# Sums of the middle norm behind the last product, two weight splits earlier, and the pre-FFN norm's steps one slot later, in a streaming encoder layer

## The chip, the cores and the metric

The kernel runs on one core of a Trainium2 chip. The core has a matrix engine (PE, with its weight loads listed apart as PEld), a vector engine (DVE), a scalar engine (ACT), a further engine called POOL, and SP, which only issues the DMAs here. Each engine takes its own instructions in a fixed order and waits on semaphores for the others. The metric is the device time of one execution in microseconds (us); lower is better.

## The reference, cut to what matters

One layer of a hybrid encoder runs on 256 + 64 = 320 tokens with 2048 features. The change lies between the output projection of the mixer and the up-projection of the feed-forward part:

```
x = x + rmsnorm(jnp.concatenate([a_out, b_out], axis=-1) @ w_out, g_post_mix)
h = rmsnorm(x, g_pre_ffn)
gu, ffn_buf = causal_dwconv(h @ w_up, ffn_buf, w_ffn_dw, b_ffn_dw)
gate, up = jnp.split(gu, 2, axis=-1)
x = x + rmsnorm((jax.nn.silu(gate) * up) @ w_down, g_post_ffn)
```

`rmsnorm` divides each token by the root of the mean of its squares over the 2048 features and multiplies by a gain per feature.

## The kernel before

**Layout.** Features lie on the 128 partitions, tokens along the free dimension (T = 320), so the 2048 features are 16 blocks of 128 x 320. Each fp32 weight tile `w` is split in two: ACT casts it to `whi` (L217), DVE subtracts to get `wlo` (L218), and the same is done with the activations. A product is three matmuls: `whi` with the high part of x, `whi` with its low part, `wlo` with the high part (L233, L234, L237 in `block_matmul`; L1067 to L1069 in `second`). Loaded tiles `w` rotate through three buffers (`wst`), so a load waits until the `wlo` of the load three earlier is done; the split tiles rotate through three pairs (`wsp`).

**Output projection.** Its contraction of 16 blocks is cut in 11 + 5. The first 11 of output blocks 0 to 14 are done before the region of the change. The loop that begins at L1084 then goes through output blocks n = 0 to 15: it loads and splits the 640 columns of `w_out2` for the block, runs 15 matmuls (`second`), and `evacuate` adds the result to `m[n]` on DVE (L1080), squares it on ACT into `sq` (L1040), multiplies by the gain g2 on ACT (L1083), and adds `sq` to the running sum `acc` on DVE (L1042). Block 15, the last product, is done whole: 33 matmuls from two loads of `w_out1` (768 and 640 columns) and 15 from `w_out2`, 48 in all. Its own square is not added to `acc`; it stays in `sq`.

**Up-weight sets.** The first up-projection group (`up_group`, L1163) needs eight sets of weights, each a load of 128 x 1024 with a split. Three of them are loaded inside the loop (`upr`, at n in (3, 6, 10)) and split inside it (`upw`, at n in (6, 10, 14)); the split is placed, on ACT and on DVE, behind that engine's newest instruction from the split of the same block's `w_out2`. Those loads have two buffers of their own, the split tiles three. Five more sets follow behind the loop.

**Mid norm.** `rstd([acc, last])` sums over the partitions with matmuls that have the data as weights and a column of ones as moving operand: three for `acc` and three for `sq` (L259; each is two passes in the trace). DVE (L264) and POOL (L265) make the reciprocal root, `rstd_rows` spreads it over the partitions (L272), and `keep_warm` puts dummy matmuls (L280) around that. Then DVE and ACT update x1 and make the two parts of the next input block by block.

**Other norm.** The norm before the feed-forward part is applied behind the up-projection, to its result. `second_norm` is a job of two steps: the sums of `acc` (16 squares of x1), and then `rb2`, the spread root, which ACT copies out of PSUM (L1178). Jobs advance at every 20th matmul that `block_matmul` counts; `start(second_norm(), 68, 1)` makes the first step due 68 matmuls on, and the second is due 12 after it. The first seven up-projection results wait in PSUM for `rb2`: four from `up_group`, and blocks 2, NFB + 2 and 3 (48 matmuls each) that PE runs meanwhile. DVE empties them with L1195 and L1196 into `fbuf`.

**What sets the order.** A scheduler lays out each engine's instructions at build time, by priorities (`tc.high_priority`) and by a model of when operands are ready; `tc.issue_after(i)` holds what is in its scope behind instruction i. At run time the order on each engine is fixed.

Of the kernel before, what the change touches and what calls it, by code (L numbers as in the profile page):

```python
# [17 lines left out]
P = 128  # L18
# [4 lines left out]
T = TP + TS  # L23
# [77 lines left out]
def trunk_kernel(ctx, tc, ins, outs):  # L101
    nc = tc.nc
    V, S, G, PE = nc.vector, nc.scalar, nc.gpsimd, nc.tensor
# [32 lines left out]
    def start(gen, wait, g=0, t=0):  # L136
        job = [dense[1] + wait, gen, g, t, []]
        jobs.append(job)
        return job
# [5 lines left out]
    def newest(engine, n0):  # L145
        return next((i for i in reversed(nc.cur_bb.bb.instructions[n0:]) if i.engine == engine), None)
# [45 lines left out]
    def pv(name, a=None, b=None):  # L192
        o, w = PAR[name]
        if a is None:
            return par[:, o:o + w]
        return par[:, o + a:o + (a + 1 if b is None else b)]

    def cv(name, n=P, m=P):
        o, _ = CST[name]
        return cst[0:n, o:o + m] if o < NCST1 else cst2[0:n, o - NCST1:o - NCST1 + m]  # L200
# [20 lines left out]
    def load_split(src, width, pool=None):  # L221
        with tc.high_priority(offset=boost[0]):
            return split_w(load_dma(src), width, pool)

    def block_matmul(ps, src, rhs, nks, final=True, first=True):
        nk = sum(nks)
        k0 = 0
        for nk_part in nks:
            hi, lo = load_split(src[:, k0 * P:(k0 + nk_part) * P], nk_part * P)
            for j in range(nk_part):  # L230
                xh, xl = rhs(k0 + j)
                wh = hi[:, j * P:(j + 1) * P]
                tick(PE.matmul(ps, wh, xh, start=(first and k0 + j == 0), stop=False))  # L233
                tick(PE.matmul(ps, wh, xl, start=False, stop=False))  # L234
            for j in range(nk_part):
                xh, xl = rhs(k0 + j)
                tick(PE.matmul(ps, lo[:, j * P:(j + 1) * P], xh, start=False, stop=(final and k0 + j == nk - 1)))  # L237
            k0 += nk_part
# [15 lines left out]
    def rstd(accs, pool=None, between=None):  # L254
        pool = pool or ps_g
        pst = pool.tile([P, 512], F32, tag=pool.name[-1], name="pst")
        for i, a in enumerate(accs):
            for c, o in enumerate((0, 128, 192)):
                mm = PE.matmul(pst[:, c:c + 1], a[:, o:o + P], cv("ones", P, 1), start=(i == 0 and c == 0),  # L259
                          stop=(i == len(accs) - 1), skip_group_check=True)  # L260
            if between is not None:
                between(i, mm)
        rr = small.tile([P, 3], F32, tag="rr", name="rr")
        V.tensor_scalar(rr, pst[:, 0:3], 1.0 / D, EPS, ALU.mult, ALU.add)  # L264
        G.tensor_tensor(rr, rr, nhalf[:, 0:3], ALU.pow)  # L265
        return rr, mm
# [30 lines left out]
    def hx(k):  # L297
        return hi_t[k], lo_t[k]
# [17 lines left out]
    with tc.tile_pool(name="xp", bufs=1) as xp:  # L316
# [25 lines left out]
        with tc.high_priority(offset=PRI_E):  # L342
            keep_warm(psw, NWARM)

            last = {}
# [42 lines left out]
        for k0 in range(0, KB, 2):  # L388
            hi, lo = pre[k0 // 2]
            for ks in ((k0,), (k0 + 1,)) if k0 < 4 else ((k0, k0 + 1),):  # L390
                for wt in (hi, lo):
                    for k in ks:
                        for i, b in enumerate(FIRST):
                            ps = ready[b][:, 0:T]
                            o = (k - k0) * FW + i * P
                            w = wt[:, o:o + P]
                            xh, xl = hx(k)
# [4 lines left out]
        def first_norm():  # L402
            rr, _ = rstd([ssum[:, 0, :], ssum[:, 1, :]])
            yield 36, 1, 0
            S.copy(rb, rstd_rows(rr)[0])

        job = start(first_norm(), 24, 1)
# [598 lines left out]
    def bx(k):  # L1006
        return b_hi[KORDER[k]], b_lo[KORDER[k]]

    m = []
    for n in range(KB - 1):  # L1010
        psm = ps_p.tile([P, 512], F32, tag="p", name="psm")
# [15 lines left out]
    acc = None  # L1027
# [23 lines left out]
    def up_load(kk, pool=None):  # L1051
        with tc.high_priority(offset=boost[0]):
            return load_dma(up_src[:, :, kk * 256:(kk + 1) * 256], pool)

    def up_split(w, pool=None):
        with tc.high_priority(offset=boost[0]):
            return split_w(w, HALF, pool)

    upw, upr = [], []
    nk2 = KB - K1  # L1060

    def second(n, psm, w, js):
        hi, lo = w
        for j in js:
            xh, xl = bx(K1 + j)
            o = j * P
            PE.matmul(psm, hi[:, o:o + P], xh, start=(j == 0 and n < KB - 1), stop=False)  # L1067
            PE.matmul(psm, hi[:, o:o + P], xl, start=False, stop=False)
            PE.matmul(psm, lo[:, o:o + P], xh, start=False, stop=(j == nk2 - 1))  # L1069

    last = held = None

    def evacuate(n, psm, whole):
        nonlocal last, held
        with tc.high_priority(offset=PRI_E):
            if whole:
                m.append(act.tile([P, T], F32, tag=f"hl{n}", name=f"m{n}"))
                src = psm[:, 0:T]
            else:
                V.tensor_tensor(m[n], m[n], psm[:, 0:T], ALU.add)  # L1080
                src = m[n]
            last = square_acc(n, src)
            held = S.activation(m[n], src, AF.Identity, scale=pv("g2", n)).ins  # L1083

    opened = {}
    for n in range(KB):
        with ExitStack() as e:
            if n == 2:
                e.enter_context(tc.issue_after(flush))
            mark = len(nc.cur_bb.bb.instructions)  # L1090
            w2 = load_split(ins["w_out2"][n], nk2 * P)
        if n in (3, 6, 10):
            upr.append(up_load(len(upr), urp))
        if n in (6, 10, 14):
            with ExitStack() as e:
                for x in (mybir.EngineType.Activation, mybir.EngineType.DVE):
                    e.enter_context(tc.issue_after(newest(x, mark)))
                upw.append(up_split(upr[len(upw)], ugp))
        nc.sync.dma_start(x1[:, n:n + 1, :], ins["x"][:, n:n + 1, :])
        if n == KB - 1:  # L1100
            nc.sync.dma_start(fpar, ins["fpar"])
        whole = n == KB - 1
        pool = (ps_p, ps_t)[n // 2 % 2]
        psm = pool.tile([P, 512], F32, tag=pool.name[-1], name="psm2")
        if whole:
            block_matmul(psm[:, 0:T], ins["w_out1"][n], bx, (6, 5), False)
        if n == 0:
            opened[0] = psm, w2
            second(n, psm[:, 0:T], w2, range(nk2 - 1))
            continue  # L1110
        if n == 1:
            second(n, psm[:, 0:T], w2, range(nk2 - 1))
            second(0, opened[0][0][:, 0:T], opened[0][1], (nk2 - 1,))
            second(n, psm[:, 0:T], w2, (nk2 - 1,))
        else:
            second(n, psm[:, 0:T], w2, range(nk2))
        for n, psm in ((0, opened[0][0]), (1, psm)) if n == 1 else ((n, psm),):
            evacuate(n, psm, whole)
    boost[0] = 0
# [1 line left out]
    hi2, lo2 = [], []  # L1121
    with tc.high_priority(offset=PRI_E):
        psw = ps_p.tile([P, 512], F32, tag="p", name="psw")
        rr, mm = rstd([acc, last])
        keep_warm(psw, 5, mm)
        rb1, mm = rstd_rows(rr)
        keep_warm(psw, 10, mm)
        split = None
        for k in range(KB):
            if k % 2 == 1 and 1 < k < 13:  # L1130
                with ExitStack() as e:
                    if k < 7:
                        e.enter_context(tc.issue_after(split))
                        e.enter_context(tc.issue_after(held))
                    upw.append(up_split(up_load(len(upw))))
            with ExitStack() as e:
                if 0 < k < 4:
                    e.enter_context(tc.issue_after(added))
                V.tensor_tensor(m[k], m[k], rb1, ALU.mult)
            added = V.tensor_tensor(x1[:, k, :], x1[:, k, :], m[k], ALU.add).ins  # L1140
            g = pv("g3", k)
            hi2.append(act.tile([P, T], F32R, tag=f"hh{k}", name=f"hi2_{k}"))
            lo2.append(act.tile([P, T], F32R, tag=f"hl{k}", name=f"lo2_{k}"))
            S.activation(hi2[k], x1[:, k, :], AF.Identity, scale=g)
            split = V.scalar_tensor_tensor(lo2[k], x1[:, k, :], g, hi2[k].bitcast(F32), ALU.mult, ALU.subtract).ins
# [29 lines left out]
    def second_norm():  # L1175
        rr, _ = rstd([acc])
        yield 12, 1, 0
        S.copy(rb2, rstd_rows(rr)[0])  # L1178

    boost[0] = PRI_W  # L1180
    job = start(second_norm(), 68, 1)
    for b in (2, NFB + 2, 3):
        first[b] = ps_g.tile([P, 512], F32, tag="g", name="psu")
        block_matmul(first[b][:, 0:T], ins["w_up"][2 * (b % NFB) + b // NFB], hx2, (8, 8))
# [60 lines left out]
    with tc.high_priority(offset=PRI_E):  # L1245
        last = square_acc(KB - 1, held_y[:, 0:T])
# [13 lines left out]
    rr, mm = rstd([acc, last], ps_p, lambda i, mm: residuals(2 * i, mm))  # L1260
    rb3, mm = rstd_rows(rr, ps_p)
# [10 lines left out]
    for step in PLAN_Y.split():  # L1272
        how, ks = step[0], step[1:]
        n = 2 if len(ks) == 4 else 1
# [96 lines left out]
```

## Time and profile before

| what | value |
|---|---|
| median of three runs | 1484.64 us (1484.1 to 1485.72) |
| the profiled execution | 1484.99 us |
| its span, first to last instruction | 1483.2 us, so 1.79 us lie around it |
| granted PE clock, mean | 0.999 of full speed |
| DVE, ACT, POOL busy | 67%, 49%, 15% of the span |
| HBM read, written | 215.33 MB, 7.12 MB |

The profile has a page of sums and the trace behind it. A row of the timeline gives the start, the duration, the engine, the line of the kernel, the operation, the tiles (out<-in), the shape and a count of like instructions that are merged in the row; in brackets stands how long the engine was idle before and who ended it. Matmuls are pipelined: a row of 0.31 us overlaps the next, so the distance between starts is what a matmul costs. In the chain of waits, a row is start, duration and piece.

### The profile page before, as it was taken

How to read it: one execution, taken by the hardware profiler on the slowest of the kernel's cores; microseconds unless marked ns; L12 is line 12 of the kernel's file. 1: busy time of each engine (PE TensorE's matmuls, PEld its weight loads, DVE VectorE, ACT ScalarE, POOL GpSimd, SP SyncE). 2: the span in 40 equal slices, each digit the busy share in tenths (PEclk: the TensorE clock that was granted, in tenths of full speed). 3: DMA queues.
4: the chain of work that ended last, by engine and by line, in shares of the span. 5: the costliest groups of instructions: out<-in, count | busy, mean ns of one | idle time of the engine just before them, and what ended most of it. 6: DMA issues, size and time to landing. Idle time of an engine off the chain costs nothing.

```text
span 1483.2 us, 27308 instructions
## 1 busy us (share of the span) xinstructions
PE 1474.4 (99%) x10625; PEld 1454.0 (98%) x10626; DVE 993.7 (67%) x1812; ACT 731.9 (49%) x1355; POOL 229.0 (15%) x390
## 2 busy tenths in 40 slices
PE   9999999999999999999999999999999999999998
PEld 9999999999999989999999999999999999999997
DVE  6779888889988778765346666445666445666554
ACT  7674656655554746544334444334444334444453
POOL 0110101021010001322002222002322001223101
PEclk9999999999999999999999999999999999999999
DMA  8435453545445734444554444454444455444453
GB/s 295 140 115 155 158 162 114 153 150 149 127 126 172 231 107 143 157 145 130 149 174 146 153 151 127 146 163 164 147 150 140 137 150 172 148 156 143 136 148 119
DMA packets 98281, 224.22 MB, mean 151 GB/s; under 512 B 18792, under 2 KB 39528, under 8 KB 98152
## 3 DMA queue, kind: packets, MB, share of 16 engines
q1 hardware_dynamic: 98008, 222.45, 47.3%
q8 instruction: 83, 1.36, 0.4%
q14 instruction: 46, 0.38, 0.1%
q10 hardware_dynamic: 144, 0.03, 0.0%
HBM read 215.33 MB, written 7.12 MB: 150 GB/s over the span
## 4 chain that ended last, share of the span: by engine, by line
PE 95%; DVE 2%; ACT 2%; issue 1%; DMA 1%; POOL 0%; DVEq 0%; ACTq 0%; POOLq 0%
PE psu L237 13%; PE psu L234 13%; PE psu L233 13%; PE psdn L233 7%; PE psdn L234 7%; PE psdn L237 7%; PE psq L233 3%; PE psq L234 3%; PE psq L237 3%; PE psu L1163 2%; PE psm L237 2%; PE psm L233 2%; PE psm L234 2%; PE psv L233 1%; PE psgate L233 1%; PE psgate L237 1%
## 5 line engine op out<-in xcount | busy, mean ns | idle before, releaser
L217 ACT CAST whi<-w 128x1024 fp32r<-128x1024 f32 (+2 forms) x440 | 412.4, 940 | 481.7 <-PE psu L234 166.2
L218 DVE TENSOR_TENSOR wlo<-w,whi 128x1024 fp32r<-128x1024 f32 (+2 forms) x440 | 476.7, 1084 | 191.5 <-ACT whi L217 122.3
L233 PE MATMUL psu<-hi,whi 128*128 128x320 f32 x1344 | 397.0, 309 | 0.0
L234 PE MATMUL psu<-lo,whi 128*128 128x320 f32 x1344 | 396.9, 309 | 0.0
L233 PEld LDWEIGHTS psu<-hi,whi 128*128 128x128 f32 x1344 | 252.3, 188 | 0.0
L234 PEld LDWEIGHTS psu<-lo,whi 128*128 128x128 f32 x1344 | 252.3, 188 | 0.0
L237 PE MATMUL psu<-hi,wlo 128*128 128x320 f32 x1344 | 224.4, 309 | 0.0
L237 PEld LDWEIGHTS psu<-hi,wlo 128*128 128x128 f32 x1344 | 203.9, 188 | 0.0
L234 PE MATMUL psdn<-gl,whi 128*128 128x320 f32 x660 | 195.9, 310 | 0.0
L1197 POOL COPY nffn<-fbuf 128x2 f32<-128x2 f32 x88 | 100.5, 1142 | 586.8 <-DVE fbuf L1195 583.7
L1195 DVE TENSOR_TENSOR fbuf<-psu,rb 128x256 f32<-128x256 f32 x88 | 37.3, 424 | 169.0 <-PE psu L237 169.0
L233 PE MATMUL psdn<-gh,whi 128*128 128x320 f32 x480 | 142.8, 309 | 0.0
L234 PEld LDWEIGHTS psdn<-gl,whi 128*128 128x128 f32 x660 | 123.9, 188 | 0.3
L233 PE MATMUL psq<-hh,whi 128*128 128x320 f32 x352 | 105.9, 314 | 0.0
L234 PE MATMUL psq<-hl,whi 128*128 128x320 f32 x352 | 104.1, 309 | 0.0
L233 PEld LDWEIGHTS psdn<-gh,whi 128*128 128x128 f32 x480 | 90.1, 188 | 0.0
L237 PE MATMUL psdn<-gh,wlo 128*128 128x320 f32 x480 | 89.9, 309 | 0.0
L237 PEld LDWEIGHTS psdn<-gh,wlo 128*128 128x128 f32 x480 | 75.3, 188 | 0.0
L233 PEld LDWEIGHTS psq<-hh,whi 128*128 128x128 f32 x352 | 66.1, 188 | 0.5 <-issue 0.2
L234 PEld LDWEIGHTS psq<-hl,whi 128*128 128x128 f32 x352 | 66.1, 188 | 0.2
L563 DVE SCALAR_TENSOR_TENSOR cvt<-ub,par,cvt 128x320 f32<-128x320 f32 x120 | 65.2, 544 | 0.1
L1240 DVE TENSOR_TENSOR y<-y,psdn 128x320 f32<-128x320 f32 x45 | 22.0, 488 | 58.7 <-PE psdn L237 58.7
(356 smaller groups left out, 2473.8 us busy)
## 6 DMA issues: line engine op xcount, KB each, us to landing
w<-in_w_up SPq DMA_DIRECT2D x176, 512.0 KB
w<-in_w_in SPq DMA_DIRECT2D x88, 512.0 KB
w<-in_w_down SPq DMA_DIRECT2D x64, 384.0 KB
w<-in_w_down SPq DMA_DIRECT2D x64, 320.0 KB
w<-in_w_out SPq DMA_DIRECT2D x32, 320.0 KB
w<-in_w_out SPq DMA_DIRECT2D x16, 384.0 KB
w<-in_w_first SPq DMA_DIRECT2D x6, 512.0 KB
wtp<-wsp SPq DMA_DIRECT2D x4, 640.0 KB
```

The source lines that it names most:

```text
L217: S.copy(hi[:, 0:width], w[:, 0:width])
L218: V.tensor_tensor(lo[:, 0:width], w[:, 0:width], hi[:, 0:width].bitcast(F32), ALU.subtract)
L233: tick(PE.matmul(ps, wh, xh, start=(first and k0 + j == 0), stop=False))
L234: tick(PE.matmul(ps, wh, xl, start=False, stop=False))
L237: tick(PE.matmul(ps, lo[:, j * P:(j + 1) * P], xh, start=False, stop=(final and k0 + j == nk - 1)))
L563: return lambda: V.scalar_tensor_tensor(acc, x, w, acc, ALU.mult, ALU.add)
L1163: PE.matmul(pss[i][:, 0:T], wt[:, o:o + P], x, start=(k == 0 and n == 0), stop=(k == KB - 1 and n == 2))
L1195: V.tensor_tensor(buf[:, 2:258], psu[:, 0:TP], rb2[:, 0:TP], ALU.mult)
L1197: G.tensor_copy(nffn[:, b, 0, :], buf[:, 256:258])
L1240: V.tensor_tensor(y[:, n, :], y[:, n, :], psd[:, 0:T], ALU.add)
```

## The change

Three edits. The first sums of the mid norm (those of `acc`) are held behind the last matmul of the last product. The third load inside the loop moves from n = 10 to 9, the second and third split from n = 10 and 14 to 9 and 12. The other norm's first step is due 84 matmuls on and not 68.

```diff
@@ in second(n, psm, w, js)
-            PE.matmul(psm, lo[:, o:o + P], xh, start=False, stop=(j == nk2 - 1))
+            mm = PE.matmul(psm, lo[:, o:o + P], xh, start=False, stop=(j == nk2 - 1))
+        return mm
@@ in the loop over n
-        if n in (3, 6, 10):
+        if n in (3, 6, 9):
             upr.append(up_load(len(upr), urp))
-        if n in (6, 10, 14):
+        if n in (6, 9, 12):
...
-            second(n, psm[:, 0:T], w2, range(nk2))
+            mm = second(n, psm[:, 0:T], w2, range(nk2))
@@ the mid norm
-        rr, mm = rstd([acc, last])
+        with tc.issue_after(mm.ins):
+            rr, mm = rstd([acc, last])
@@ the other norm
-    job = start(second_norm(), 68, 1)
+    job = start(second_norm(), 84, 1)
```

**First place: PE, in the last product (`psm_6790`) and at its end.** The difference, in which `pst` is the PSUM tile of the mid norm's sums:

```order
 L237 MATMUL psm_6790<-bh_2360,wlo 128x320
 L237 MATMUL psm_6790<-bh_3468,wlo 128x320
-L259 MATMUL pst<-cst,acc 128x1 x3
 L237 MATMUL psm_6790<-bh_4386,wlo 128x320
 L237 MATMUL psm_6790<-bh_4977,wlo 128x320
@@ -3200,4 +3199,5 @@
 L1068 MATMUL psm_6790<-bl_6325,whi 128x320
 L1069 MATMUL psm_6790<-bh_6324,wlo 128x320
+L259 MATMUL pst<-cst,acc 128x1 x3
 L259 MATMUL pst<-cst,sq 128x1 x3
```

The three sums of `acc` leave their place behind the 14th of the last product's 48 matmuls and stand behind the 48th, directly ahead of the sums of `sq`.

**Second place: ACT, in the loop, around the third set.** `m_6037`, `m_6089`, `m_6150`, `m_6216` are the results of blocks 9, 10, 11 and 12; a cast of 128x640 is a block's `w_out2`, that of 128x1024 the third up-weight set. Before:

```order
L1083 ACTIVATE m_6089<-m_6089,par 128x320
L217 CAST whi<-w 128x640
L217 CAST whi<-w 128x1024
L1040 ACTIVATE sq<-m_6150 128x320
L1083 ACTIVATE m_6150<-m_6150,par 128x320
L217 CAST whi<-w 128x640
L1040 ACTIVATE sq<-m_6216 128x320
L1083 ACTIVATE m_6216<-m_6216,par 128x320
L217 CAST whi<-w 128x768
```

Now:

```order
L217 CAST whi<-w 128x640
L217 CAST whi<-w 128x1024
L1040 ACTIVATE sq<-m_6037 128x320
L1084 ACTIVATE m_6037<-m_6037,par 128x320
L217 CAST whi<-w 128x640
L1040 ACTIVATE sq<-m_6089 128x320
L1084 ACTIVATE m_6089<-m_6089,par 128x320
L217 CAST whi<-w 128x640
L1040 ACTIVATE sq<-m_6150 128x320
L1084 ACTIVATE m_6150<-m_6150,par 128x320
L217 CAST whi<-w 128x640
L1040 ACTIVATE sq<-m_6216 128x320
```

The third set's cast stands two blocks earlier: behind the cast of `w_out2` of block 12, ahead of the square of block 9. Between the set and the first cast of the last product (128x768) there are four squares now, and two before. DVE's `wlo` rows move in the same way, and the second set's stand one block earlier on both engines. On SP, the load of `fpar` (128x528) moves ahead of the `w_out2` load of block 13; no other load changes its place.

**Third place: PE and ACT, at the other norm.** The rows with `hi_8` and up to `hi_15` in them end block NFB + 2, those from `hi_0` begin block 3. PE before:

```order
L233 MATMUL psu<-hi_14_7002,whi 128x320
L259 MATMUL pst<-cst,acc 128x1 x3
L234 MATMUL psu<-lo_14_7003,whi 128x320
L233 MATMUL psu<-hi_15_7008,whi 128x320
L234 MATMUL psu<-lo_15_7009,whi 128x320
L237 MATMUL psu<-hi_8_6954,wlo 128x320
```

PE now:

```order
L237 MATMUL psu<-hi_13_6996,wlo 128x320
L237 MATMUL psu<-hi_14_7002,wlo 128x320
L237 MATMUL psu<-hi_15_7008,wlo 128x320
L259 MATMUL pst<-cst,acc 128x1 x3
L233 MATMUL psu<-hi_0_6888,whi 128x320
L234 MATMUL psu<-lo_0_6889,whi 128x320
```

The sums stand 11 matmuls later, at the end of block NFB + 2. The spread (`psb`, L272) stood at that end; it now stands 20 matmuls behind the sums, inside block 3. ACT around the copy of `rb2`, before:

```order
L1040 ACTIVATE sq<-x_6336 128x320
L217 CAST whi<-w 128x1024
L1178 COPY rb_6855<-psb 128x320
L1199 ACTIVATE cg<-fbuf_7012,fpar 128x322
L1199 ACTIVATE cu<-fbuf_7013,fpar 128x322
L217 CAST whi<-w 128x1024
```

ACT now:

```order
L1040 ACTIVATE sq<-x_6336 128x320
L217 CAST whi<-w 128x1024 x2
L1180 COPY rb_6855<-psb 128x320
L1201 ACTIVATE cg<-fbuf_7012,fpar 128x322
L1201 ACTIVATE cu<-fbuf_7013,fpar 128x322
```

One more weight cast stands ahead of the copy now. On DVE, the `wlo` that stood directly behind the other norm's `rr` (L264) stands directly ahead of it.

## The prediction, as it was put on record

> **What bounds the kernel now.** I read the page first, then the chain of waits, then the timeline of PE around each edit.
>
> ```profile
> PE 95%; DVE 2%; ACT 2%; issue 1%; DMA 1%; POOL 0%; DVEq 0%; ACTq 0%; POOLq 0%
> ...
> 624.43 1.17 PE psu L237 x8
> 627.95 1.17 PE psu L237 x8
> ```
>
> The first line, from the page, gives the chain that ends last by engine: 95% of it is PE. So a change is worth what it takes from PE's waits and from PE's own instructions on that chain. The other two, from the chain in order of time, give the cost of one matmul: the groups begin 24 matmuls apart (8 of L237, 16 of L233 and L234), and 3.52 us / 24 = 0.147 us. Any larger distance between two starts is a loss. Behind 583 us PE's timeline keeps this pace up to the last norm, so what PE gains before 583 us it keeps to the end. The losses that the edits can reach are four.
>
> The first is inside the last product:
>
> ```profile
> 523.32 0.46 PE L237 MATMUL psm<-bh,wlo 128*128 128x320 f32 x2
> 524.39 0.83 PE L259 MATMUL pst<-cst,acc 128*128 128x1 f32 x6 [0.62 <-DVE acc L1042]
> 525.08 0.68 PE L237 MATMUL psm<-bh,wlo 128*128 128x320 f32 x3
> 525.75 0.31 PE L233 MATMUL psm<-bp,whi 128*128 128x320 f32 x1
> ```
>
> PE reaches the sums of `acc` and waits for DVE. From 523.32 to 525.75 stand six matmuls (two, three, and one that I leave out), 0.88 us of work; it took 2.43 us. **1.55 us** are lost: about 0.78 of waiting, 0.69 for the six passes, 0.08 for getting back to pace.
>
> The second and third are waits for split weights, at the start of the last product and inside block 11:
>
> ```profile
> 520.73 0.31 PE L1069 MATMUL psm<-bh,wlo 128*128 128x320 f32 x1
> 521.46 0.41 PE L233 MATMUL psm<-bh,whi 128*128 128x320 f32 x1 [0.42 <-ACT whi L217]
> ...
> 521.85 0.31 PE L233 MATMUL psm<-bh,whi 128*128 128x320 f32 x1
> ...
> 512.03 0.31 PE L1068 MATMUL psm<-bl,whi 128*128 128x320 f32 x1
> ...
> 512.52 0.31 PE L1067 MATMUL psm<-bp,whi 128*128 128x320 f32 x1
> ```
>
> From 520.73 to 521.85 are three steps, 0.44 us, and it took 1.12: **0.68** lost to ACT's cast of the first part of `w_out1`. From 512.03 to 512.52 are two steps in 0.49 us: **0.20** lost, to the `wlo` of block 11.
>
> The fourth is at the other norm's sums:
>
> ```profile
> 576.43 0.31 PE L233 MATMUL psu<-hi,whi 128*128 128x320 f32 x1
> 576.97 0.83 PE L259 MATMUL pst<-cst,acc 128*128 128x1 f32 x6 [0.23 <-DVE acc L1042]
> 577.66 0.39 PE L234 MATMUL psu<-lo,whi 128*128 128x320 f32 x1
> ```
>
> The sums begin 0.54 us behind the matmul ahead of them, so **0.39** is waiting; their own 0.69 us stays wherever they stand.
>
> **The change part by part. First edit: the sums of `acc` behind the last product.** The 1.55 us inside the product go. In exchange six passes stand between the last matmul and the sums of `sq`. Those wait for ACT's square anyway, and the end of the kernel has the same sequence already in the new form:
>
> ```profile
> 530.00 0.31 PE L1069 MATMUL psm<-bh,wlo 128*128 128x320 f32 x1
> 530.84 0.83 PE L259 MATMUL pst<-cst,sq 128*128 128x1 f32 x6 [0.53 <-ACT sq L1040]
> ...
> 1467.39 0.60 PE L237 MATMUL psy<-gp,wlo 128*128 128x320 f32 x3
> 1467.83 0.72 PE L259 MATMUL pst<-cst,acc 128*128 128x1 f32 x6
> 1468.52 0.83 PE L259 MATMUL pst<-cst,sq 128*128 128x1 f32 x6
> ```
>
> In the middle, without the passes between, the sums of `sq` start 0.84 us behind the last matmul. At the end the third matmul of its row starts at 1467.39 + 2 x 0.147 = 1467.68, the six passes of `acc` follow, and those of `sq` start at 1468.52: again 0.84. The square hides the six passes. If it hid none, 0.69 us would come back; I take 0. `acc` itself was ready at 524.39, and the last product ends past 527 in any case: no new wait. Gain **1.55**, at least 0.86.
>
> **Second edit: the sets.** No instruction is added; two splits move, by one block and by two, the load for the third moves in the code but not in SP's order, and on SP `fpar` passes the `w_out2` load of block 13. What bounds this stage is how far DVE and ACT lag behind PE:
>
> ```profile
> 510.60 0.48 DVE L1042 TENSOR_TENSOR acc<-acc,sq 128x320 f32<-128x320 f32 x1
> 512.13 0.48 DVE L1042 TENSOR_TENSOR acc<-acc,sq 128x320 f32<-128x320 f32 x1
> ...
> 511.52 0.47 ACT L1040 ACTIVATE sq<-m 128x320 f32<-128x320 f32 x1 [0.51 <-DVE m L1080]
> 513.11 0.47 ACT L1040 ACTIVATE sq<-m 128x320 f32<-128x320 f32 x1
> ...
> 500.48 1.22 DVE L218 TENSOR_TENSOR wlo<-w,whi 128x1024 fp32r<-128x1024 f32 x1
> 501.62 0.48 DVE L1080 TENSOR_TENSOR m<-m,psm 128x320 f32<-128x320 f32 x1
> ```
>
> A block costs DVE 1.53 us and ACT 1.59 when they run without a break, and PE 15 x 0.147 = 2.20. So each block makes good 0.6 us of lag, and a set, 1.14 us on DVE, costs two blocks. The chain shows that lag at the last product:
>
> ```profile
> 515.87 1.67 ACT whi L217 x2
> ...
> 519.62 0.48 ACT sq L1040
> ...
> 520.59 0.82 ACT whi L217
> ```
>
> The pair at 515.87 is the cast of block 14's `w_out2` and the third set; from there DVE and ACT hand work to each other without a pause until the cast that PE waits for, at 520.59. PE wants it done at 520.88 - 0.20 = 520.68, so begun by 519.84: it is 0.75 too late. With the set two blocks earlier there are two more blocks to recover in, 1.2 us, which puts the cast near 519.4. Going through the new order step by step, with the distances that these engines kept in the trace, I get 511.75 for the third set, 513.66, 515.85 and 517.44 for the casts of blocks 13 to 15 and 519.2 for this one (an estimate): 0.6 us to spare. The second set falls into a hole:
>
> ```profile
> 507.75 1.68 ACT L217 CAST whi<-w 128x640 fp32r<-128x640 f32 x2 [1.42 <-DMA w<-in_w_out]
> ```
>
> ACT idles 1.42 us there for a load; now the set's cast fills that time, and the `wlo` of block 11, behind which the set no longer stands, is done more than 1 us before PE needs it. The cast also needs its load:
>
> ```profile
> 514.09 3.70 SPq L210 DMA_DIRECT2D w<-in_w_out  x3
> ...
> 515.00:518.50 3.50, 3.50 (x26) 3.50 (x25) 3.21 (x5) 3.44 (x7) 0.00 (x0) 1.00 0.71 204
> ```
>
> The three issues are block 15's 320 KB, then 384 KB and 320 KB of `w_out1`. From 515.0 to 518.5 the DMAs moved 3.5 x 204 = 714 KB, as much as the first two together (721 in the same unit), so the 384 KB were in shortly behind 518.5. In the new order its issue stays at about 515.6, behind the `wlo` of block 13. Gain 0.68 + 0.20 = **0.88**; with the load late, as in the first rival, nothing.
>
> **Third edit: the other norm's steps.** The sums move behind 11 more matmuls, 1.6 us; `acc` was ready at 576.97 and PE now asks at 576.58 + 1.61 = 578.2. Gain **0.39**; 0 if DVE is later than before. The spread stands 20 matmuls behind the sums, 2.9 us, time in which DVE and POOL finish `rr` even with a `wlo` ahead of it on DVE (rows of the last rival). PE's count of instructions is the same.
>
> **Sum.** 1.55 + 0.88 + 0.39 = 2.82 us. The profiled execution took 1484.99, so 1482.17; it lies 0.35 above the median of the three runs, so against that median 1484.64 - 2.82 = **1481.8**, 0.19% less.
>
> **The rivals.** *The last product's weights stay late.* `fpar`, 264 KB, now goes ahead of block 13's load:
>
> ```profile
> 502.87 4.80 DMA w<-in_w_out
> ...
> 509.36 0.33 SPq L210 DMA_DIRECT2D w<-in_w_out  x1
> ...
> 509.00:513.80 4.80, 4.80 (x33) 4.60 (x32) 4.45 (x8) 4.19 (x9) 0.02 (x1) 1.00 0.83 275
> ```
>
> At 275 GB/s those 270 kB take 0.98 us. A `w_out2` load has taken up to 4.80 us under such traffic; with 0.98 more, block 13's would land at 515.1, 1.5 us behind my step for its cast. The casts behind it then slip by 0.85 us, and the issue of the 384 KB, which waits for that block's `wlo`, by 1.0; of the 0.88, 0.3 to 0.7 come back. Against it: the burst ended near 513.8 with both loads in it, so in either order the later one is in by then. Time 1482.1 to 1482.5, about 1482.4; chance 0.20. The Trainium skill, page "DMA: Bandwidth & Descriptors", section "Queues, rings and completion order", says that each DMA engine consumes descriptors in ring order; by that rule block 13's load stands behind all of `fpar`, which speaks for this rival, and no row here shows the two apart.
>
> *The sets collide.* They stand three blocks apart now and not four; three blocks make good 1.8 us, a set costs 1.14 on DVE, but if a load also makes ACT wait there, PE waits at block 13 or 14 instead, and with a later `acc` the 0.39 may go too. Only the first edit counts then: 1484.64 - 1.55 = 1483.1; chance 0.12.
>
> *Slower: the copy of `rb2` comes too late.* The seven results in PSUM are freed only behind it.
>
> ```profile
> 578.38 1.05 ACT L217 CAST whi<-w 128x1024 fp32r<-128x1024 f32 x1 [2.76 <-PE psu L234]
> 579.88 0.43 ACT L1178 COPY rb<-psb 128x320 f32<-128x320 f32 x1 [0.45 <-PE psb L272]
> ...
> 580.75 0.42 DVE L1195 TENSOR_TENSOR fbuf<-psu,rb 128x256 f32<-128x256 f32 x1
> ...
> 586.73 0.31 PE L233 MATMUL psu<-hi,whi 128*128 128x320 f32 x1
> ```
>
> At 586.73 PE begins the block that needs the first of those banks again. DVE freed it at about 581.4. In the new order the spread comes at 581.9 by the old clock, and ACT has one more cast ahead of the copy, which waits for PE to finish with a `whi` tile at about 581.6 and takes 1.05: the copy starts near 582.6 and the bank is free near 583.7, 2.6 us ahead of PE (586.73 - 0.39 = 586.3). PE begins to wait if the copy slips by 2.6 us more, and the kernel is slower than before once it slips by 2.6 + 2.8 = 5.4. Only a weight load that holds up the extra cast could do that; with as much as 8 us of slip the time is 1487. Chance 0.04.
>
> **How the numbers follow.** The forecast, all three gains, has 0.64 and its own range 1481.0 to 1482.5, since single runs before lie from 0.54 below to 1.08 above their median. The range takes in the first rival and the second, with some of that spread: 1481.0 to 1483.5. A measurement of this kernel can tell about 0.2%, 2.97 us, from no change, which puts the bound at 1481.67, only 0.13 below the forecast. Nearly half of the forecast's chance lies beyond it: faster 0.30, the rest and the two middle rivals make the same 0.66, slower 0.04.
>
> **What would show it.** In the profile of the changed kernel: no wait in the last product and six passes of `acc` right behind its last matmul, with the sums of `sq` still 0.84 behind that matmul (first edit); the first matmul of the last product 0.147 behind block 14 (second edit; if not, the row names ACT or a DMA, and that decides between the first two rivals); the other norm's sums 0.147 behind the L237 ahead of them; the block of 586.73 without a wait and 2.8 us earlier. I am wrong if any of these waits stands, or if PE shows a new one above 0.2 us before 600 us.

## The result and the profile after

| what | before | after |
|---|---|---|
| median of 13 runs each | 1484.74 us (1483.92 to 1485.89) | 1481.83 us (1481.32 to 1482.82) |
| profiled execution, its span | 1484.99, 1483.2 us | 1481.38, 1479.6 us |

The ratio is 0.9981, 95% interval 0.9973 to 0.9988: 2.91 us less. The predicted time was 1481.8. The interval lies wholly below 1: the gain is clear of no change, and far below 2%.

The chain that ends last, by engine, from the page of the changed kernel:

```profile
PE 97%; ACT 1%; DVE 1%; DMA 0%; POOL 0%; issue 0%; SPq 0%; DVEq 0%
```

It was 95% PE before, and behind it is a change of kind: between 495 and 520 us the chain of before ran through loads, ACT and DVE, and in this execution of the changed kernel it runs through PE's matmuls alone. The timeline of PE at the four places of the prediction (start, duration, engine, line, operation, tiles, shape, count):

```profile
519.79 0.31 PE L1069 MATMUL psm<-bh,wlo 128*128 128x320 f32 x1
519.93 0.37 PE L233 MATMUL psm<-bh,whi 128*128 128x320 f32 x1
520.15 0.31 PE L234 MATMUL psm<-bl,whi 128*128 128x320 f32 x1
...
521.75 0.90 PE L237 MATMUL psm<-bh,wlo 128*128 128x320 f32 x5
...
526.89 0.31 PE L1069 MATMUL psm<-bh,wlo 128*128 128x320 f32 x1
527.03 0.72 PE L259 MATMUL pst<-cst,acc 128*128 128x1 f32 x6
527.72 0.83 PE L259 MATMUL pst<-cst,sq 128*128 128x1 f32 x6
...
573.91 1.34 PE L237 MATMUL psu<-hi,wlo 128*128 128x320 f32 x8
575.09 0.72 PE L259 MATMUL pst<-cst,acc 128*128 128x1 f32 x6
...
581.95 1.34 PE L237 MATMUL psu<-hi,wlo 128*128 128x320 f32 x8
583.12 0.31 PE L233 MATMUL psu<-hi,whi 128*128 128x320 f32 x1
```

The last product begins 0.14 behind block 14. No pass stands among its L237, where the sums of `acc` were. The sums of `sq` start 0.83 behind its last matmul, with the six passes of `acc` in between. The other norm's sums start 8 x 0.147 = 1.18 behind the row of eight, at pace, and so does the block that needs the first bank again.

**Where 3.6 us of span went.** The profiled spans differ by 3.6, more than the medians. Part of it arose 300 us ahead of the change, in a stage that both kernels run in the same order. PE of before, then of after, there:

```profile
188.49 0.31 PE L233 MATMUL psq<-hh,whi 128*128 128x320 f32 x1
...
197.94 1.16 PE L908 MATMUL ks<-sn,kq 128*128 128x128 f32 x8
```

```profile
188.50 0.31 PE L233 MATMUL psq<-hh,whi 128*128 128x320 f32 x1
...
197.30 1.05 PE L908 MATMUL ks<-sn,kq 128*128 128x128 f32 x8
```

Level at 188.5, 0.64 apart at 197.9. The kernel of run 3 below, which differs from the one before only behind the last product, takes 8.80 us between these two rows, as the changed kernel does: chance of one execution, not the change. From there to the bank the difference grows from 0.64 to 586.73 - 583.12 = 3.61, so **2.97** belongs to the stages of the change. By place: at the last matmul of block 14 it is 520.73 - 519.79 = 0.94, so 0.30 up to there (predicted 0.20, block 11); at the end of the last product 530.00 - 526.89 = 3.11, of which 0.62 at its start (three steps took 1.12 before, and now 0.14 + 0.22 + 0.14; predicted 0.68) and 1.55 inside (predicted 1.55); then 0.50 (predicted 0.39) from there to the bank.

Two waits of ACT in the changed kernel's trace matter below:

```profile
507.08 0.73 ACT L217 CAST whi<-w 128x640 fp32r<-128x640 f32 x1 [0.83 <-DMA w<-in_w_out]
...
519.00 0.83 ACT L217 CAST whi<-w 128x768 fp32r<-128x768 f32 x1 [0.30 <-DMA w<-in_w_out]
```

The first is the load of block 10, late here as it was before (1.42). The second is the last product's first cast: it did not wait for ACT's other work but for its load, and PE's second matmul came 0.07 late behind it. The prediction had given this cast 0.6 us to spare; it had none.

### The profile page after: what moved, and what is told of

It reads as the page before. It is cut to its first block, busy times and chain, and to the rows that moved or that the text cites. A ratio compares the mean times of both kernels' runs of the same rounds, so it can differ in the third digit from the quotient of the medians.

```text
span 1479.6 us, 27305 instructions
## 1 busy us (share of the span) xinstructions
PE 1472.6 (100%) x10626; PEld 1453.6 (98%) x10626; DVE 993.6 (67%) x1812; ACT 732.0 (49%) x1355; POOL 232.5 (16%) x390
## 4 chain that ended last, share of the span: by engine, by line
PE 97%; ACT 1%; DVE 1%; DMA 0%; POOL 0%; issue 0%; SPq 0%; DVEq 0%
PE psu L233 13%; PE psu L237 13%; PE psu L234 13%; PE psdn L233 7%; PE psdn L234 7%; PE psdn L237 7%; PE psq L233 3%; PE psq L234 3%; PE psq L237 3%; PE psu L1165 2%; PE psm L233 2%; PE psm L237 2%; PE psm L234 2%; PE psv L233 1%; PE psgate L233 1%; PE psgate L237 1%
## 5 line engine op out<-in xcount | busy, mean ns | idle before, releaser
L237 PE MATMUL psu<-hi,wlo 128*128 128x320 f32 x1344 | 224.7, 309 | 0.0
L237 PEld LDWEIGHTS psu<-hi,wlo 128*128 128x128 f32 x1344 | 204.0, 188 | 0.0
L237 PE MATMUL psdn<-gh,wlo 128*128 128x320 f32 x480 | 89.9, 309 | 0.0
L237 PEld LDWEIGHTS psdn<-gh,wlo 128*128 128x128 f32 x480 | 75.3, 188 | 0.0
```

## The experiments

Differences of medians are against the kernel before, timed together with the run; their 95% intervals are the run's, turned into us with 1484.5. A comparison of two variants has an interval from resampling the executions of each (11 per kernel).

**1 to 3. Each edit alone.** The diffs are the three parts of the change shown above: the sums behind the last product; the two lists of block numbers; 84 for 68.

> The first edit alone: the sums of acc behind the last product, sets and other norm as before. Theory: 1.55 us less than before (about 1483.2 against 1484.74); no wait and no pass of acc inside the last product, the sums of sq still 0.84 us behind its last matmul, and the stalls of 0.68 us (first matmul of the last product), 0.20 us (block 11) and 0.39 us (other norm) still there. Rival A, the six passes are not hidden: the sums of sq start 1.5 us behind the last matmul and only 0.86 us are gained. Rival B, the wait for acc only moves on to the next product of the same queue: less than 1 us in all.

> The second edit alone: sets split behind blocks 6, 9, 12; the sums of acc stay inside the last product. Theory: 0.88 us less than before (about 1483.9); the first matmul of the last product 0.15 us behind block 14, no loss in block 11, but PE still waits about 0.8 us for acc inside the last product, since PE and the adds of acc both come 0.9 us earlier; the three edits add up. Rival, the wait for acc was the lateness of the same DVE chain: with the sets earlier it goes as well, and this edit alone brings 1.6 us, the first edit on top of it then only 0.8.

> The third edit alone: the other norm's first step due 84 matmuls on. Theory: 0.39 us less than before (about 1484.35), the sums of the other norm 0.15 us behind the matmul ahead of them, and no wait at the block that needs the first PSUM bank again. Rival: the gain is given back at that bank or at the copy, 0.

| kernel | median | less than before (1484.52) | interval |
|---|---|---|---|
| sums only | 1482.97 | 1.55 | 0.7 to 3.4 |
| sets only | 1483.55 | 0.97 | -0.4 to 2.2 |
| start only | 1484.13 | 0.39 | -1.0 to 1.6 |

The three add up to 2.91, what the whole change brought; with intervals this wide, a sum that comes out to the hundredth is luck. Only the first is clear of no change by time; for the others the traces decide. In the kernel with the sums alone, the sums stand as in the changed kernel (0.84 between the last matmul and those of `sq`), and the other waits are still there:

```profile
521.01 0.42 PE L233 MATMUL psm<-bh,whi 128*128 128x320 f32 x1 [0.27 <-ACT whi L217]
...
528.01 0.31 PE L1069 MATMUL psm<-bh,wlo 128*128 128x320 f32 x1
528.16 0.72 PE L259 MATMUL pst<-cst,acc 128*128 128x1 f32 x6
528.85 0.83 PE L259 MATMUL pst<-cst,sq 128*128 128x1 f32 x6
...
574.98 0.83 PE L259 MATMUL pst<-cst,acc 128*128 128x1 f32 x6 [0.23 <-DVE acc L1042]
```

With the sets alone, PE still waits for `acc` inside the last product, so the first edit keeps its whole worth (the rival of that run falls). The expectation's other half was missed there: that profile, of the run's slowest execution (1485.54), loses 0.52 in block 10 and 0.28 at the start of the last product, behind a wait of ACT of 2.01 for block 10's load. And with the start alone the other norm's sums come at pace, 8 x 0.147 behind their row of eight. The kernel with the sets alone, then the one with the start alone:

```profile
524.93 0.83 PE L259 MATMUL pst<-cst,acc 128*128 128x1 f32 x6 [0.61 <-DVE acc L1042]
```

```profile
577.76 1.33 PE L237 MATMUL psu<-hi,wlo 128*128 128x320 f32 x8
578.93 0.72 PE L259 MATMUL pst<-cst,acc 128*128 128x1 f32 x6
```

**4 to 7. Which of the two sets.** Changed kernel, with one or both splits back:

```diff
-        if n in (6, 9, 12):
+        if n in (6, 9, 14):
```

This is run 4; run 5 is the changed kernel itself, run 6 has (6, 10, 12) there, and run 7 has (6, 10, 14) with the loads at (3, 6, 10) as before.

> The changed kernel with the third set split behind block 14 again (6, 9, 14); the load of fpar stays ahead of the one of block 13. Theory (lag of ACT and DVE): PE waits about 0.7 us at the start of the last product and the row names ACT's cast; no loss in block 11; about 0.7 us more than the changed kernel. Rival (the load of the first part of w_out1 sets that cast): the stall is under 0.3 us or its cast waits for a DMA.

> The changed kernel once more, beside the next three, to have a time and a second profile of it from the same chip. With the third set back at block 14 it lost nothing (1481.68 us, with a loss of 0.20 us at the start of the last product), so the 0.68 us that I put on the third set's move is in doubt. Time as before, 1481.8; if the losses that hang on loads differ from one execution to the next, this profile shows other ones than the first (first matmul of the last product 0.06 late, block 11 none).

> The changed kernel with the second set split behind block 10 again (6, 10, 12); the load of fpar then stands behind block 13's again. Theory now: the second set's move into ACT's wait for a load is what takes the lag away, and the third's does nothing alone; so this one loses about as much as both moves gained, 0.7 to 0.9 us more than the changed kernel, with sets two blocks apart. Rival, the theory of the prediction: only block 11's 0.20 comes back and the last product starts on time. Rival, either move alone is enough: no difference.

> The changed kernel with the loads and splits of the sets as before (loads at 3, 6, 10, splits at 6, 10, 14): first and third edit together. All theories: 0.9 us more than the changed kernel (about 1482.7), by the sum 1.55 + 0.39 below the kernel before. If it is as fast as the changed kernel, the sets were worth nothing with the sums of acc out of the way.

| median, us | third set at 12 | third set at 14 |
|---|---|---|
| second set at 9 | 1481.74 (run 5) | 1481.68 (run 4) |
| second set at 10 | 1483.34 (run 6) | 1482.35 (run 7) |

Run 4 was timed apart from the other three, but the kernel before agrees (1484.52 beside run 4, 1484.53 beside the others). The third set's move alone, behind the second at 10, **costs** 0.99 (0.29 to 1.40); behind the second at 9 it changes nothing. The second set's move by one block is the gain: 0.61 (0.11 to 1.16) is what both moves bring in the full kernel, and with the third set left at 14 it is all there (0.67 between runs 7 and 4, 0.24 to 1.14). In run 4 the cast that PE waits for in the kernel before is not late by 0.7 with the third set back. PE of that run:

```profile
520.29 0.31 PE L1069 MATMUL psm<-bh,wlo 128*128 128x320 f32 x1
520.53 0.42 PE L233 MATMUL psm<-bh,whi 128*128 128x320 f32 x1
```

0.24 to the first matmul of the last product, so 0.09 lost, where the kernel before has 0.73 and loses 0.58. With the second set at 10, SP also issues `fpar` behind block 13's load and not ahead of it; run 9 below holds that load back alone, behind block 15's, and is no slower for it, so the place of `fpar` doesn't explain what run 6 loses. Run 6's profile was of an execution of 1481.40, far below that kernel's median; run 8 is a second one.

**8. The second set at 10, third at 12, once more.**

> The changed kernel with the second set behind block 10 (6, 10, 12) for a second profile: the first was of its fastest execution, 1481.40, where the median is 1483.34. Theory: a common execution shows 1.5 to 2 us of loss in blocks 9 to 13 or at the last product, where a late w_out2 load meets the second set's split, and the third set's split, two blocks on, holds the next ones up as well. Rival: no such loss, and the time is lost elsewhere.

This one took 1482.71. ACT, then PE:

```profile
506.94 1.68 ACT L217 CAST whi<-w 128x640 fp32r<-128x640 f32 x2 [2.76 <-DMA w<-in_w_out]
...
520.39 0.83 ACT L217 CAST whi<-w 128x768 fp32r<-128x768 f32 x1 [0.77 <-DMA w<-in_w_out]
```

```profile
511.46 0.42 PE L1069 MATMUL psm<-bh,wlo 128*128 128x320 f32 x1 [0.35 <-DVE wlo L218]
...
521.27 0.42 PE L233 MATMUL psm<-bh,whi 128*128 128x320 f32 x1 [0.72 <-ACT whi L217]
```

ACT waited 2.76 for block 10's load, with the second set's cast in the pair behind it, and PE, by the distances between its starts, loses 0.61 in block 11, 0.32 in block 13 and 0.97 at the last product. At the last product the cast waits for its load, which SP cannot issue before DVE has done block 13's `wlo`, and that stands behind both sets.

The next table has, for every run, three times, each from the profiled execution: the wait of ACT for block 10's load; the time from the start of block 10's cast to the start of the last product's first cast, with what ACT waited of it for that cast's own load in brackets; and PE's loss from 500 to 524 us (what the distances between starts have above 0.147, added up).

| sets at | ACT waits, us | cast to cast, us | PE loses, us |
|---|---|---|---|
| 6, 10, 14 (before; runs 1, 3, 7) | 1.42; 1.93, 2.88, 1.08 | 12.84; 12.85, 12.85, 12.99 | 0.87; 0.53, 2.49, 0.69 |
| 6, 10, 12 (runs 6, 8) | 1.51, 2.76 | 12.76, 13.45 (0.77) | 0.24, 1.91 |
| 6, 9, 14 (run 4) | 1.27 | 11.67 | 0.54 |
| 6, 9, 12 (after; runs 2, 5, 9) | 0.83; 2.01, 1.22, 1.83 | 11.92 (0.30); 11.74 (0.15), 11.49, 11.97 (0.38) | 0.05; 0.80, 0.00, 1.34 |
| 6, 9, 12 (runs 10, 11, 12) | 0.89, 1.50, 0.77 | 11.58, 11.66, 12.01 (0.40) | 0.05, 0.86, 0.25 |

The third column shows the cause. Less the brackets it is 12.68 to 12.99 with the second set at 10 and 11.49 to 11.67 with it at 9, whether the third set stands at 12 or at 14. ACT of runs 7, 6, 4 and 5, in this order:

```profile
506.79 1.68 ACT L217 CAST whi<-w 128x640 fp32r<-128x640 f32 x2 [1.08 <-DMA w<-in_w_out]
...
519.78 0.82 ACT L217 CAST whi<-w 128x768 fp32r<-128x768 f32 x1
```

```profile
506.25 1.68 ACT L217 CAST whi<-w 128x640 fp32r<-128x640 f32 x2 [1.51 <-DMA w<-in_w_out]
...
519.01 0.84 ACT L217 CAST whi<-w 128x768 fp32r<-128x768 f32 x1
```

```profile
507.99 0.73 ACT L217 CAST whi<-w 128x640 fp32r<-128x640 f32 x1 [1.27 <-DMA w<-in_w_out]
...
519.66 0.82 ACT L217 CAST whi<-w 128x768 fp32r<-128x768 f32 x1
```

```profile
507.11 0.73 ACT L217 CAST whi<-w 128x640 fp32r<-128x640 f32 x1 [1.22 <-DMA w<-in_w_out]
...
518.60 0.82 ACT L217 CAST whi<-w 128x768 fp32r<-128x768 f32 x1
```

In runs 7 and 6 the pair of casts is block 10's and the second set's, both behind the wait; in runs 4 and 5 the set's cast stands ahead of the wait and fills part of that time. The difference of about 1.2 us is near the 1.14 that a set costs DVE. And in the chain of waits of the kernel before, no piece from the landing of block 10's load at 507.67 to the cast at 520.59 belongs to PE or to a DMA: it is ACT's and DVE's work throughout. So a set between the two is paid for in full, and the third set is between them at 12 as at 14.

What PE loses in the end depends on when that load lands too, and that changes from one execution to the next: with the new order, runs 9 and 11 waited 1.83 and 1.50 and still lost 1.34 and 0.86. With waits near 1.1, run 7 lost 0.69 and run 5 nothing; PE of run 7 (run 5 has no such row):

```profile
520.65 0.41 PE L233 MATMUL psm<-bh,whi 128*128 128x320 f32 x1 [0.43 <-ACT whi L217]
```

**9 and 10. The loads around it.** In run 9 `fpar` is held behind the three `w_out2` loads of blocks 13 to 15; in run 10 the loads of x for blocks 12 to 15 and `fpar` are held behind the last product's two loads. In the first diff, `loaded` is block 15's `w_out2` load.

```diff
-            nc.sync.dma_start(fpar, ins["fpar"])
+            with tc.issue_after(loaded):
+                nc.sync.dma_start(fpar, ins["fpar"])
```

```diff
-        nc.sync.dma_start(x1[:, n:n + 1, :], ins["x"][:, n:n + 1, :])
+        if n < 12:
+            nc.sync.dma_start(x1[:, n:n + 1, :], ins["x"][:, n:n + 1, :])
...
+            with tc.issue_after(newest(mybir.EngineType.SP, mark)):
+                for k in range(12, KB):
+                    nc.sync.dma_start(x1[:, k:k + 1, :], ins["x"][:, k:k + 1, :])
+                nc.sync.dma_start(fpar, ins["fpar"])
```

> The changed kernel with the load of fpar (264 KB) held back behind the three w_out2 loads of blocks 13 to 15. Theory (the load order costs nothing, the first rival of the prediction): no difference in time within 0.3 us; block 13's load lands 0.3 to 1.0 us earlier. Rival: fpar ahead of block 13 costs 0.3 to 0.7 us, so this is faster by that. Rival: the first load of w_out1 now shares the DMAs with fpar and lands later, the last product's first cast waits for it, up to 1 us slower.

> The changed kernel with the loads of x for blocks 12 to 15 (four of 160 KB) and of fpar (264 KB) held back behind the loads of w_out1 for the last product: 900 KB less in the burst in which the w_out2 loads of blocks 10 to 13 take up to 4.8 us. Theory now (what PE loses in blocks 9 to 11 and at the last product is set by when those loads land, and differs from one execution to the next): faster than the changed kernel by 0.3 to 0.7 us, about 1481.2, with a narrower spread, and no loss of PE between 505 and 527 us. Rival (the lag of DVE and ACT alone sets it): 1481.7. Rival (the loads come too late for the up-projection's sets): over 1482.5, with PE waiting in the up-projection's first group.

Run 9: 1481.43, 0.31 below the changed kernel of run 5, with an interval from 0.72 below to 0.05 above: it can't be told from no difference, and its profile shows no cause (it is of an execution of 1482.27, in which ACT waited 1.83 for block 10's load). Run 10: 1481.43 too, 2.93 below the kernel before timed with it (1484.36), where the changed kernel had 2.79 and 2.91. Its profiled execution loses 0.05 from 500 to 524 us, but so did the changed kernel's. The thinner burst is neither shown to help nor to harm; no wait in the up-projection's first group came of it.

**11. Twice the passes of `acc`.**

```diff
-            rr, mm = rstd([acc, last])
+            rr, mm = rstd([acc, acc, last])
```

> The changed kernel with the three sums of acc made twice behind the last product, twelve passes and not six (so acc counts twice in the mid norm). Theory: ACT's square hides the first six and none of the other six; the sums of sq start 0.147 + 2 x 0.69 = 1.53 us behind the last matmul, 0.69 more than with six. Rival: part of the square's time covers more passes, under 0.6; or the six were not hidden either, then 0.69 as well but the square long ready.

The run is one execution, of 1483.92 us. PE:

```profile
527.23 0.31 PE L1069 MATMUL psm<-bh,wlo 128*128 128x320 f32 x1
527.37 1.39 PE L259 MATMUL pst<-cst,acc 128*128 128x1 f32 x12
528.63 0.81 PE L259 MATMUL pst<-cst,sq 128*128 128x1 f32 x6
```

The sums of `sq` come 1.40 behind the last matmul: 0.57 more than with six passes, not 0.69. Twelve passes take 1.26, so six take 0.63 or less, and 0.14 + 0.63 is just inside the 0.83 that the square needs. The cover holds six passes and hardly more. (The run shows something else too; see the last section.)

**12. The spread 4.3 us later.**

```diff
-    job = start(second_norm(), 84, 1)
+    job = start(second_norm(), 124, 1)
```

> The changed kernel with the other norm's first step due 124 matmuls on, which puts the spread at the very end of block 3, 4.3 us later. Theory (margin of the copy of rb2 3.0 us in the changed kernel, the bank needed at 583.12): PE waits for the bank behind the spread, from the spread to the first results taken out 1.4 us less its own 0.33: 1.1 us lost, once, and 1482.9. Rival: the later order of DVE and ACT makes the next blocks wait as well, over 2 us. Rival: the bank isn't what PE waits for, no loss.

PE, then DVE:

```profile
583.19 0.54 PE L272 MATMUL psb<-cst,rr 128*128 128x128 f32 x3
585.22 0.39 PE L233 MATMUL psu<-hi,whi 128*128 128x320 f32 x1 [1.48 <-DVE fbuf L1198]
```

```profile
583.38 1.22 DVE L218 TENSOR_TENSOR wlo<-w,whi 128x1024 fp32r<-128x1024 f32 x1 [1.17 <-PE psu L237]
584.52 0.42 DVE L1197 TENSOR_TENSOR fbuf<-psu,rb 128x256 f32<-128x256 f32 x1
```

In the changed kernel DVE is done with the first bank here:

```profile
580.04 0.21 DVE L1198 TENSOR_TENSOR fbuf<-psu,rb 128x64 f32<-128x64 f32 x1
```

The bank is free there at 580.25, and PE wants it at 583.12: a margin of 2.87. In run 12 the wait is where the slower rival of the prediction put it and has its name: PE waits for DVE to empty the first bank. From the spread to the next matmul 2.03 us; less the spread's own 0.33, 1.7 are lost, more than the 1.1 expected: a `wlo` stood ahead on DVE until 584.52. The loss comes once: the block at 585.22 begins 2.10 behind that of the changed kernel, of which 0.34 were there at the last product's end, and at the last norm the distance is still 2.14 (sums of `acc` at 1466.37 and 1464.23). So the rival by which the next blocks wait as well falls. The median is 1483.80, 0.56 below the kernel before (1484.36), with an interval that holds zero (-0.7 to 1.9): most of the change's gain is gone.

## Why the prediction was right, and where its steps were not

- **First edit, 1.55:** right in size and cause. Alone it brought 1.55; the wait and the six passes inside the product are gone, the distance to the sums of `sq` stayed at 0.83, and run 11 shows that the square covers these six passes and little beyond.
- **Second edit, 0.88:** the sum was right (0.97 alone, 0.61 beside the other edits, 0.30 + 0.62 in the profiled pair), the cause was not. The step that failed reads: with the third set "two blocks earlier there are two more blocks to recover in, 1.2 us". The third set's place is worth nothing once the second stands at 9, and moving it alone costs 0.99. What counts is the other half of the edit, to which I gave only block 11's 0.20: the second set's cast goes into ACT's wait for block 10's load instead of behind it, and the last product's first cast follows block 10's 1.2 us sooner (third column of the table). The prediction began the unbroken work of ACT and DVE at 515.87, with the third set; its own trace has it from 507.75, and there is nothing to recover for a set that moves within it. That the term's size came out all the same is luck: the 1.2 us that the third set was to win back happen to be what the second set's move takes off.
- **The cast with 0.6 us to spare:** wrong. My step of 519.2 counted ACT's and DVE's own work; in the profile ACT was ready and waited 0.30 for the load. The kernel got by with a loss of 0.07.
- **Third edit, 0.39:** the wait is gone from every profile with the sums at 84, and was there in those with 68 (0.39 in runs 1 and 2). The time agrees (0.39), though its interval holds zero.
- **First rival (`fpar` ahead of block 13's load):** its burden can't be excluded: holding `fpar` back gave 0.31, with zero at the edge of the interval. That is at the lower end of the 0.3 to 0.7 that I put on it. If it is real, the likeliest case already contained it.
- **Second rival (sets collide):** not with (6, 9, 12), but run 6 is that case: sets two blocks apart behind a late load, 1.60 (0.90 to 2.05) slower than the changed kernel, and run 8 has the wait at block 13 that this rival named (0.32). That the new lists avoid it was not clear from one trace.
- **Slower rival (copy of `rb2`):** not here; the margin is 2.87 us, where the prediction had 2.6. Run 12, with the spread 4.3 us later, pays for it.

What stays open: how much of the spread between executions comes from block 10's load alone. The few profiles of each order don't settle it, and no run took the third set's own load, which SP issues just ahead of block 10's, out of its way. Why the third set at 12 makes (6, 10, 12) slower than (6, 10, 14) rests on run 8's profile alone; run 6's, of its fastest execution, shows no such loss.

## What to carry to other kernels

When two moves are made in one edit, try each alone even if the sum comes out: here one of them was worth the whole gain and the other nothing, and on its own a loss. Put extra work where the engine already waits for a load, not behind that wait. And compare two profiles stage by stage: 0.64 of the 3.6 us between these spans came from a stage that nobody had touched.

## What the runs showed of the hardware

The granted clock of PE fell at the mid norm in run 11, and there in no other profile; ten of those have the twelve passes of the changed kernel. The busy time by engine in two stretches (PE, PEld, DVE, ACT, POOL, then the granted clock, the DMA share and GB/s), of run 11 and of the changed kernel:

```profile
526.00:530.00 4.00, 4.00 (x33) 3.64 (x32) 0.16 (x1) 2.43 (x4) 0.28 (x1) 1.00 0.12 40
530.00:532.00 2.00, 1.92 (x8) 0.92 (x7) 0.49 (x1) 1.25 (x2) 0.56 (x1) 0.67 0.00 0
532.00:536.00 4.00, 4.00 (x16) 2.07 (x15) 3.93 (x10) 2.77 (x6) 0.00 (x0) 0.74 0.00 0
```

```profile
530.00:532.00 2.00, 2.00 (x12) 0.98 (x11) 1.62 (x4) 1.55 (x3) 0.00 (x0) 1.00 0.00 0
532.00:536.00 4.00, 4.00 (x28) 3.70 (x26) 4.00 (x9) 2.13 (x5) 0.00 (x0) 1.00 0.00 0
```

PE counts as busy for all of the 4 us ahead of the drop, yet the clock falls: half of that time (527.37 to 529.30) are passes with one column of moving data. The groups that follow show it:

```profile
530.62 0.86 PE L272 MATMUL psb<-cst,rr 128*128 128x128 f32 x3
531.27 3.73 PE L280 MATMUL psw<-wz 128*128 128x512 bf16 x10
534.65 1.12 PE L1165 MATMUL psu<-hi,whi 128*128 128x320 f32 x4
```

```profile
529.74 0.54 PE L272 MATMUL psb<-cst,rr 128*128 128x128 f32 x3
530.11 2.32 PE L280 MATMUL psw<-wz 128*128 128x512 bf16 x10
532.08 1.12 PE L1165 MATMUL psu<-hi,whi 128*128 128x320 f32 x4
```

From the spread to the up-projection run 11 (above) needs 4.03 us and the changed kernel (below) 2.34: 1.69 lost to the clock, three times what the six passes themselves cost. The means of 0.67 and 0.74 fit a clock at half for about 3.4 us (0.33 x 2 / 0.5 + 0.26 x 4 / 0.5), and between 531 and 534 us the trace has 0.50. The Trainium skill, page "TensorE: Matmul & The Clock Gate", section "Part 1: The HAM clock gate (the "warmup" mystery)", says that the array falls to half its rate behind an idle window of about 3.4 us. The trace has the half rate, but no idle time of PE stood ahead of it. It is one execution, so whether six more such passes always do this is open, and no run tells the one-column passes from other reasons for the drop. What it does show is that a row of PE that counts as busy is no proof of a full clock.
